# A softmax that streams through one core: three loads of 32 rows for six of 16, two stores of 32 rows, and VectorE's steps in another order

## The chip, the core and the metric

The kernel runs on one core of one Trainium2 chip. The metric is device time in microseconds (us); a kernel's time is the median of its runs. Of the core's engines, VectorE (DVE in the profile), ScalarE (ACT) and GpSimd (POOL) compute here, and SyncE's queue (SPq) issues all transfers between device memory (DRAM) and the on-chip memory (SBUF). TensorE isn't used.

## The reference

Softmax over the last axis of x, which has the shape 16 x 1024 x 512 in float32:

```python
x_max = np.max(x, axis=-1, keepdims=True)
exp_x = np.exp(x - x_max)
return exp_x / np.sum(exp_x, axis=-1, keepdims=True)
```

These are 16,384 independent rows of 512 elements. x has 33.55 MB and the output as much; both must cross the DMA engines once, 67.11 MB in all.

## The kernel before

**Tiling.** Each of the 128 partitions handles 128 rows, numbered 0 to 127 in each partition. Eight rows of all partitions make a *group* (`GROUP`, 128 x 4096 elements, 2.10 MB), so there are 16 groups, g = 0 to 15, and group g has the rows 8g to 8g + 7. The SBUF tensor `held` has room for 96 rows per partition, 12 groups (`RING`); rows 96 to 127 reuse the places of rows 0 to 31. All work is done in place in `held`.

**Transfers.** `BLOCKS` (line 21) says how rows in DRAM are dealt to partitions: in a block of n rows per partition, partition p has n consecutive rows of DRAM, which is n x 2 KB in one run. Before, each block has 16 rows, and so each DMA moves 16 rows of all partitions: 4.19 MB in 128 runs of 32 KB. `ORDER` (line 22) is SyncE's program, a list written by hand: "L" is a load (line 126) and "S" a store (line 152). SyncE does it strictly in this order. The first `AHEAD` entries, six loads, are issued at once (lines 133 to 135; `AT_HEAD` puts the first of them ahead of the start barrier). The rest (lines 139 to 154) wait before they are issued:

- a store waits until all groups in its rows are scaled (semaphores `scaled`, one per group);
- a load into reused places waits until every store that reads these places has landed (`stored`, one per store).

All DMAs go through one queue, in the order of their issue. A DMA that waits on SyncE holds back all that follow it in `ORDER`, though not those issued before it, which are still moving.

**Compute.** A group goes through four steps:

- M, on VectorE: `reduce_max` with the sign turned (line 164), 128 x 4096 to 128 x 8, after its load has landed (line 162);
- on ScalarE, in a loop over the groups in order (lines 190 to 203): eight activations of one row each, exp(x - max), in place, each with the row's sum as a by-product (line 195);
- on VectorE, once ScalarE is done with the group (line 169): the reciprocal of the eight sums (line 170);
- the multiply of the group by its reciprocals (line 172), either on GpSimd (called P) or on VectorE (called V).

`VECTOR` (line 44) is VectorE's program, again written by hand and done strictly in this order. "M5" is the max of group 5; "P5" is the reciprocal of group 5 on VectorE, and then GpSimd does the multiply; "V12" is the reciprocal and the multiply, both on VectorE. So GpSimd's multiplies come in the order of the P entries, and none starts before VectorE has reached its P entry. In before, groups 0 to 11 are scaled on GpSimd and 12 to 15 on VectorE.

Of the kernel before, what the change touches and what calls it, by code (L numbers as in the profile page):

```python
# [1 line left out]

# [4 lines left out]

F32 = mybir.dt.float32
EXP = mybir.ActivationFunctionType.Exp
AX = mybir.AxisListType.X  # L10

GROUP = 8
GROUPS = 16
RING = 12 * GROUP

BLOCKS = [(0, 16), (16, 32), (32, 48), (48, 64), (64, 80), (80, 96), (96, 112), (112, 128)]
ORDER = [
    ("L", (0, 16)),
    ("L", (16, 32)),
    ("L", (32, 48)),
    ("L", (48, 64)),
    ("L", (64, 80)),
    ("L", (80, 96)),
    ("S", (0, 16)),
    ("S", (16, 32)),  # L30
    ("S", (32, 48)),
    ("L", (96, 112)),
    ("L", (112, 128)),
    ("S", (48, 64)),
    ("S", (64, 80)),
    ("S", (80, 96)),
    ("S", (96, 112)),
    ("S", (112, 128)),
]
AHEAD = 6  # L40

VECTOR = """
    M0 M1 P0 M2 P1 M3 P2 M4 P3 M5 P4 M6 P5 M7 P6 M8 P7 M9 P8 M10 P9 M11
    P10 M12 P11 M13 V12 M14 V13 M15 V14 V15
"""

AT_HEAD = {mybir.EngineType.SP: 1}

def loads_at_the_head(nc):

    main, body = nc.main_func.blocks[0], nc.main_func.blocks[1]
    for engine, count in AT_HEAD.items():
        loads = [
            i
            for i in body.instructions
            if i.engine == engine and type(i).__name__ == "InstDMACopy"  # L60
        ][:count]
        barrier = next(
            n
            for n, i in enumerate(main.instructions)
            if i.engine == engine and type(i).__name__ == "InstDrain"
        )
        for load in loads:
            body.instructions.remove(load)
        main.instructions[barrier:barrier] = loads


@with_exitstack
def kernel(
    ctx: ExitStack,
    tc: tile.TileContext,
    x: bass.AP,
    out: bass.AP,
):
    nc = tc.nc
    nc.at_finalize(loads_at_the_head)  # L80
    P = nc.NUM_PARTITIONS

    d = x.shape[-1]
    x_rows, out_rows = x.flatten_outer_dims(), out.flatten_outer_dims()
    assert x_rows.shape[0] == GROUPS * GROUP * P

    def in_dram(rows, a, b):

        first, last = next(k for k in BLOCKS if k[0] <= a and b <= k[1])
        block = rows[first * P : last * P].rearrange("(p r) d -> p r d", p=P)  # L90
        return block[:, a - first : b - first, :]

    held = nc.alloc_sbuf_tensor("held", [P, RING, d], F32).ap()
    shift = nc.alloc_sbuf_tensor("shift", [P, GROUPS * GROUP], F32).ap()
    sums = nc.alloc_sbuf_tensor("sums", [P, GROUPS * GROUP], F32).ap()
    recip = nc.alloc_sbuf_tensor("recip", [P, GROUPS * GROUP], F32).ap()

    loads = [k for what, k in ORDER if what == "L"]
    stores = [k for what, k in ORDER if what == "S"]
    loaded = {k: nc.alloc_semaphore(f"loaded{k[0]}") for k in loads}  # L100
    scaled = [nc.alloc_semaphore(f"scaled{g}") for g in range(GROUPS)]
    stored = {k: nc.alloc_semaphore(f"stored{k[0]}") for k in stores}
    maxed = nc.alloc_semaphore("maxed")
    expd = nc.alloc_semaphore("expd")
    to_pool = nc.alloc_semaphore("to_pool")
    to_vector = nc.alloc_semaphore("to_vector")

    def take(engine, semaphore, n):

        engine.wait_ge(semaphore, n).then_inc(semaphore, -n)  # L110

    def rows(a, b):
        assert a // RING == (b - 1) // RING
        return held[:, a % RING : (b - 1) % RING + 1, :]

    def meets(k, a, b):
        return k[0] < b and a < k[1]

    def group(g):
        return g * GROUP, (g + 1) * GROUP  # L120

    def stats(t, g):
        return t[:, g * GROUP : (g + 1) * GROUP]

    def load(k):
        copy = nc.sync.dma_start(out=rows(*k), in_=in_dram(x_rows, *k))
        copy.then_inc(loaded[k], 16)
        return copy

    with tc.manual_schedule():
        for _, k in ORDER[:AHEAD]:
            tc.no_tile_sem_insts.add(load(k).ins.name)
    tc.close()
    tc.compile()  # L137

    taken, done = set(), set()
    for what, k in ORDER[AHEAD:]:  # L140
        if what == "L":
            for s in stores:
                if meets(s, k[0] - RING, k[1] - RING) and s not in taken:
                    take(nc.sync, stored[s], 16)
                    taken.add(s)
            load(k)
        else:
            for g in range(GROUPS):
                if meets(k, *group(g)) and g not in done:
                    take(nc.sync, scaled[g], 1)  # L150
                    done.add(g)
            nc.sync.dma_start(out=in_dram(out_rows, *k), in_=rows(*k)).then_inc(
                stored[k], 16
            )


    seen = set()

    def rowmax(g):
        for k in loads:  # L160
            if meets(k, *group(g)) and k not in seen:
                take(nc.vector, loaded[k], 16)
                seen.add(k)
        nc.vector.reduce_max(  # L164
            out=stats(shift, g), in_=rows(*group(g)), axis=AX, negate=True
        ).then_inc(maxed, 1)

    def scale(g, engine, ready):
        take(nc.vector, expd, 1)
        nc.vector.reciprocal(out=stats(recip, g), in_=stats(sums, g)).then_inc(ready, 1)  # L170
        take(engine, ready, 1)
        engine.tensor_mul(  # L172
            out=rows(*group(g)),
            in0=rows(*group(g)),
            in1=stats(recip, g).unsqueeze(2).to_broadcast([P, GROUP, d]),
        ).then_inc(scaled[g], 1)

    for step in VECTOR.split():
        what, g = step[0], int(step[1:])
        if what == "M":  # L180
            rowmax(g)
        elif what == "V":
            scale(g, nc.vector, to_vector)
        else:
            scale(g, nc.gpsimd, to_pool)


    nc.scalar.preload_act_table(EXP)  # L188

    with nc.scalar.Fori(0, GROUPS) as i:  # L190
        take(nc.scalar, maxed, 1)
        for r in range(GROUP):
            row = held[:, bass.ds(i % (RING // GROUP) * GROUP + r, 1), :]
            at = bass.ds(i * GROUP + r, 1)
            act = nc.scalar.activation(  # L195
                out=row,
                in_=row,
                func=EXP,
                bias=shift[:, at],
                scale=1.0,  # L200
                accum_out=sums[:, at],
            )
        act.then_inc(expd, 1)


    for k in stores:
        if k not in taken:
            take(nc.sync, stored[k], 16)


# [1 line left out]
_INS = ['x']  # L212
_OUTS = [((16, 1024, 512), 'float32')]


# [23 lines left out]
```

## Time and profile before

| what | us |
|---|---|
| median of three runs (lowest, highest) | 160.07 (159.98, 160.23) |
| the profiled execution | 160.14 |
| its span, first to last instruction or landing | 158.8 |
| busy: VectorE, ScalarE, GpSimd | 90.6, 92.0, 84.0 |

The profiled execution is 1.3 us longer than the span, for what lies around the program. A time within the profile counts from the span's start. The span doesn't end with a compute instruction but with the landing of the last store.

The trace tells for each DMA when SyncE issued it and how long it then took to land. In the order of issue (us; the numbers in brackets are the rows per partition):

| DMA | issued | issue to landing | landed |
|---|---|---|---|
| load (0,16) | 0.0 | 12.2 | 12.2 |
| load (16,32) | 0.8 | 21.1 | 21.9 |
| load (32,48) | 1.2 | 30.4 | 31.6 |
| load (48,64) | 1.6 | 39.7 | 41.3 |
| load (64,80) | 2.2 | 48.9 | 51.0 |
| load (80,96) | 2.6 | 58.8 | 61.4 |
| store (0,16) | 37.5 | 33.6 | 71.1 |
| store (16,32) | 51.5 | 29.4 | 80.9 |
| store (32,48) | 65.4 | 25.4 | 90.8 |
| load (96,112) | 71.3 | 29.0 | 100.3 |
| load (112,128) | 81.0 | 29.1 | 110.1 |
| store (48,64) | 81.5 | 38.3 | 119.8 |
| store (64,80) | 93.3 | 36.3 | 129.6 |
| store (80,96) | 112.3 | 27.1 | 139.4 |
| store (96,112) | 125.6 | 23.5 | 149.1 |
| store (112,128) | 140.9 | 17.9 | 158.8 |

Most of the time from issue to landing is spent behind the DMAs ahead in the queue. The difference of two consecutive landings is what one DMA takes of the engines.

Of the compute engines, the groups of instructions with the mean length of one:

| line, engine, step | count | mean ns |
|---|---|---|
| L164 VectorE, max of a group | 16 | 4399 |
| L195 ScalarE, Exp of one row | 128 | 712 |
| L172 GpSimd, multiply of a group | 12 | 7015 |
| L172 VectorE, multiply of a group | 4 | 4570 |
| L170 VectorE, reciprocal | 16 | 201 |

The early steps in order of time: VectorE starts M0 at 12.33, right after the first landing; ScalarE starts the Exp of group 0 at 17.11, that of group 1 at 22.76; reciprocal 0 starts at 23.00 and reciprocal 1 at 28.64; GpSimd's first multiply starts at 23.46, and eleven follow one another without a gap for 76.76 us.

In the lines of a timeline the columns are start, length, engine, line, operation and tiles with their shapes.

### The profile page before, as it was taken

What the parts mean: (1) busy time and instruction counts of PE and PEld (TensorE: products, weight loads), DVE (VectorE), ACT (ScalarE), POOL (GpSimd) and SP (SyncE); (2) the same over time, 40 slices, a digit from 0 to 9 for tenths busy, and PEclk for the clock granted to TensorE, in tenths of its full rate; (3) what the DMA queues carried; (4) which work ended last, traced back from release to release, by engine and by line L of the source; (5) the groups of instructions that cost most, each with busy time, mean ns of one, the idle gap of its engine ahead of it and who ended that gap; (6) DMA issues with size and microseconds to landing.
All of it is one profiled execution on the core that took longest, in us unless ns stands there. A gap on an engine that the chain in (4) does not pass through costs nothing. (4 is left out here: it accounts for less than half of the span.)

```text
span 158.8 us, 747 instructions
## 1 busy us (share of the span) xinstructions
DVE 90.6 (57%) x36; ACT 92.0 (58%) x257; POOL 84.0 (53%) x16
## 2 busy tenths in 40 slices
DVE  0008959777977977887700000795999998640000
ACT  0300699999999999999993000059934929200000
POOL 0000009999999999999999999259200000000000
DMA  7999999999999998999999999999999999999996
GB/s 264 470 454 396 413 487 421 396 454 470 396 396 487 437 396 380 413 396 454 470 396 421 462 437 396 446 479 396 421 446 454 396 437 473 413 404 454 446 413 264
DMA packets 2305, 67.12 MB, mean 423 GB/s; under 512 B 256, under 2 KB 256, under 8 KB 256
## 3 DMA queue, kind: packets, MB, share of 16 engines
q1 hardware_dynamic: 2304, 67.11, 98.9%
q14 instruction: 1, 0.01, 0.0%
HBM read 33.55 MB, written 33.55 MB: 423 GB/s over the span
## 5 line engine op out<-in xcount | busy, mean ns | idle before, releaser
L195 ACT ACTIVATE held<-held,shift x128 | 90.3, 712 | 40.0 <-ACTq L110 40.0
L172 POOL TENSOR_TENSOR held<-held,recip 128x4096 f32<-128x4096 f32 x12 | 83.8, 7015 | 28.0 <-POOLq L110 28.0
L164 DVE TENSOR_REDUCE shift<-held 128x8 f32<-128x4096 f32 x16 | 70.3, 4399 | 33.2 <-DVEq L110 33.2
L195 ACT ACTIVATION_READ_ACCUMULATOR held<-held,shift x128 | 24.6, 192 | 0.0
L172 DVE TENSOR_TENSOR held<-held,recip 128x4096 f32<-128x4096 f32 x4 | 18.3, 4570 | 0.6
L170 DVE RECIPROCAL recip<-sums 128x8 f32<-128x8 f32 x16 | 3.2, 201 | 16.5 <-DVEq L110 16.5
L188 ACT ACT_TABLE_LOAD x1 | 1.3, 1283 | 3.9 <-PEq L137 3.9
L223 POOL MEMSET const-float32-0.0<- 128x1 f32 x1 | 0.1, 98 | 0.2 <-issue 0.2
L223 POOL MEMSET const-uint8-127<- 128x1 uint8 x1 | 0.1, 102 | 0.0
L223 POOL MEMSET const-bfloat16-1.0<- 128x1 bf16 x1 | 0.1, 101 | 0.0
L223 POOL MEMSET const-float32-1.0<- 128x1 f32 x1 | 0.1, 98 | 0.0
## 6 DMA issues: line engine op xcount, KB each, us to landing
held<-in_x_dram SPq DMA_DIRECT2D x8, 4096.0 KB, 29.7
out_dram<-held SPq DMA_DIRECT2D x8, 4096.0 KB, 28.3
```

Source lines behind the costliest of these rows:

```text
L164: nc.vector.reduce_max(out=stats(shift, g), in_=rows(*group(g)), axis=AX, negate=True).then_inc(maxed, 1)
L170: nc.vector.reciprocal(out=stats(recip, g), in_=stats(sums, g)).then_inc(ready, 1)
L172: engine.tensor_mul(out=rows(*group(g)), in0=rows(*group(g)), in1=stats(recip, g).unsqueeze(2).to_broadcast([P, GROUP, d]),).then_inc(scal ...
L188: nc.scalar.preload_act_table(EXP)
L195: act = nc.scalar.activation(out=row, in_=row, func=EXP, bias=shift[:, at], scale=1.0, accum_out=sums[:, at],)
L223: nc = _bacc.Bacc("TRN2", target_bir_lowering=False, num_devices=1)
```

## The change

The blocks become 32 rows. The first six loads become three, of 32 rows per partition (8.39 MB in runs of 64 KB). Two stores, (0,32) and (64,96), move 32 rows each; the other four, and the two loads into reused places, keep 16 rows, which are now half of a block: per partition a run of 32 KB out of 64 KB. The bytes and the order of the rows in SyncE's queue are the same.

The semaphores follow. Store (0,32) waits for the groups 0 to 3 (before, store (0,16) waited for 0 and 1); store (64,96) waits for the groups 8 to 11. Both loads into reused places wait for store (0,32) as a whole. The first load's landing is what M0 to M3 wait for, the second that of M4 to M7, the third that of M8 to M11.

In VectorE's order, groups 3 and 10 are scaled on VectorE (V3, V10), and groups 12 and 13 on GpSimd (P12, P13). P4 stands behind V3 and P11 behind V10, and in three places two or three maxima follow one another (M0 M1 M2, M5 M6, M12 M13). GpSimd still has 12 multiplies and VectorE four. Nothing else differs; behind the shorter lists, all lines of the kernel have numbers lower by five.

```diff
-BLOCKS = [(0, 16), (16, 32), (32, 48), (48, 64), (64, 80), (80, 96), (96, 112), (112, 128)]
+BLOCKS = [(0, 32), (32, 64), (64, 96), (96, 128)]
 ORDER = [
-    ("L", (0, 16)),
-    ("L", (16, 32)),
-    ("L", (32, 48)),
-    ("L", (48, 64)),
-    ("L", (64, 80)),
-    ("L", (80, 96)),
-    ("S", (0, 16)),
-    ("S", (16, 32)),
+    ("L", (0, 32)),
+    ("L", (32, 64)),
+    ("L", (64, 96)),
+    ("S", (0, 32)),
     ("S", (32, 48)),
     ("L", (96, 112)),
     ("L", (112, 128)),
     ("S", (48, 64)),
-    ("S", (64, 80)),
-    ("S", (80, 96)),
+    ("S", (64, 96)),
     ("S", (96, 112)),
     ("S", (112, 128)),
 ]
-AHEAD = 6
+AHEAD = 3

 VECTOR = """
-    M0 M1 P0 M2 P1 M3 P2 M4 P3 M5 P4 M6 P5 M7 P6 M8 P7 M9 P8 M10 P9 M11
-    P10 M12 P11 M13 V12 M14 V13 M15 V14 V15
+    M0 M1 M2 P0 M3 P1 M4 P2 V3 P4 M5 M6 P5 M7 P6 M8 P7 M9 P8 M10 P9 M11
+    V10 P11 M12 M13 P12 M14 P13 M15 V14 V15
 """
```

## The prediction, as it was put on record before the changed kernel ran

> **What bounds it now.** I read the page's DMA rows first, then bandwidth by stretch, then SyncE's queue, and last the compute engines' timelines. Of the page:
>
> ```profile
> DMA  7999999999999998999999999999999999999996
> ...
> q1 hardware_dynamic: 2304, 67.11, 98.9%
> ...
> DVE 3%; issue 0%
> ```
>
> The DMA engines are full in every slice but the first and the last, while no compute engine is busy above 58% of the span. The third line, the chain of work that ended last, is blind here: it ends with VectorE's last multiply at 140.8 us and doesn't see that the span ends 18 us later with a store. The sum over stretches (time, DVE, ACT and POOL busy, clock, DMA share, GB/s) gives the sizes:
>
> ```profile
> 0.00:4.00 4.00, 0.00 (x0) 0.07 (x1) 0.20 (x4) 1.00 0.77 262
> 4.00:56.00 52.00, 35.90 (x14) 40.10 (x112) 32.54 (x5) 1.00 1.00 434
> 56.00:62.00 6.00, 4.56 (x2) 6.00 (x17) 6.00 (x2) 1.00 1.02 377
> 62.00:155.00 93.00, 50.12 (x20) 45.81 (x130) 45.23 (x7) 1.00 1.00 432
> ```
>
> Transfers run at 432 to 434 GB/s wherever the queue is full, so a 4.19 MB DMA takes 9.7 us and 67.11 MB take 155. The dip at 56 to 62 is the change from loads to stores: (434 - 377) x 6 / 434 = 0.8 us. So time can only be lost where SyncE's queue runs dry. When SyncE issues (start, us, count):
>
> ```profile
> 0.00 3.13 SPq L126 DMA_DIRECT2D held<-in_x_dram  x6
> 37.54 28.23 SPq L152 DMA_DIRECT2D out_dram<-held  x3
> 71.28 10.02 SPq L126 DMA_DIRECT2D held<-in_x_dram  x2
> 81.48 59.76 SPq L152 DMA_DIRECT2D out_dram<-held  x5
> ```
>
> Every DMA of before is issued long before its predecessor lands (table above): the first store at 37.5, while loads land until 61.4. That is over 20 us of cover, and it hides all compute. The price of a dry queue is in the first load: issued at 0.0 on an idle queue, it lands at 12.2, of which 9.7 is transfer. So a DMA keeps the queue full only if it is issued 2.5 us before its predecessor lands; later, it costs its lateness one for one.
>
> **The change part by part.**
>
> *Three loads for six.* Same bytes, same order. SyncE's issues fall by three (some 0.4 us each on SyncE's queue), which lay beside the first load: nothing. Two consecutive landings (71.1 and 80.9 of the first two stores) stand 9.7 us apart, which is 4.19 MB at 432 GB/s, so a boundary between queued DMAs costs nothing that shows, and five fewer boundaries gain nothing. A run of 64 KB per partition in place of 32 KB is in no row; I bound its effect at 1% of the 97 us that five 8.39 MB DMAs take, up or down (1 us), and take nothing, by the two stretches at 434 and 432.
>
> What changes is when data is usable. M0 waits for 8.39 MB, not 4.19: it starts at 12.33 + 9.7 = 22.0. The second load lands at 21.9 + 19.4 = 41.3, the third at 60.7.
>
> *VectorE's order and the merged store (0,32).* This store waits for groups 0 to 3, three on GpSimd (P0, P1, P2) and V3 on VectorE. Durations from the rows of before: a reduce starts 4.33 us after the one before it; the first Exp row follows its reduce's start by 4.8 (17.11 - 12.33); a group's reciprocal starts 5.9 us after its first Exp row (23.00 - 17.11), then one per 5.64; the multiply starts 0.46 after the reciprocal on GpSimd and 0.35 on VectorE; a GpSimd multiply takes 6.98 (76.76 / 11). So:
> M0, M1, M2 from 22.0 to 35.05; reciprocal 0 at 35.05 (ScalarE was done at 32.7, so the third reduce ahead of it costs 2.3); P0 at 35.5, P1 at 42.5, P2 from 49.46 to 56.45. M3 from 35.2; M4 waits for the second load, 41.4 to 45.8; reciprocal 2 at 45.8, in time for P2. Exp of group 3 is done in time for reciprocal 3 at 22.0 + 4.8 + 5.9 + 3 x 5.64 = 49.6, and V3 starts at 49.95: half a microsecond after P2 has begun. What VectorE's multiply costs beside GpSimd's shows once in before:
>
> ```profile
> 111.45 5.00 DVE L172 TENSOR_TENSOR held<-held,recip 128x4096 f32<-128x4096 f32 x1
> ...
> 121.04 4.43 DVE L172 TENSOR_TENSOR held<-held,recip 128x4096 f32<-128x4096 f32 x1
> ...
> 130.05 4.43 DVE L172 TENSOR_TENSOR held<-held,recip 128x4096 f32<-128x4096 f32 x1
> ```
>
> ```profile
> 105.16 7.01 POOL L172 TENSOR_TENSOR held<-held,recip 128x4096 f32<-128x4096 f32 x1 [4.94 <-POOLq L110]
> ```
>
> GpSimd's last multiply runs until 112.17. V12 starts beside it at 111.45 and takes 0.57 us more than its fellows, which have GpSimd idle; it ends 4.28 us after GpSimd's end, about its whole own length. So in the 0.72 us of overlap V12 got little or nothing done, while the reduces beside GpSimd keep their 4.4 us. I read this as V12 standing still until GpSimd is through. V3 then stands from 49.95 to 56.45 and ends at 56.45 + 4.28 to 4.43, say 60.75; the store is issued 0.1 later (as 37.54 follows the second GpSimd multiply's end, 23.46 + 2 x 6.98 = 37.42), 60.85.
>
> The Trainium skill (SBUF — State Buffer, section "Who interferes with whom") says that a VectorE instruction with two SBUF inputs and a GpSimd instruction that reads SBUF contend for one port pair, and that whichever starts first holds it for its whole instruction. The single short overlap here would also fit a slowdown in proportion, 0.57 lost of 0.72; by that, V3 would end at 59.5 and the sum would be 160.7 rather than 162.0. The lock is what I go by, since V12's end fits it within 0.15 us.
>
> The queue needed this store by 60.7 - 2.5 = 58.2. It comes 2.65 us late, and the store lands at 60.85 + 2.5 + 19.4 = 82.75, where before the same bytes had landed at 80.9. The 0.8 us of the change to stores is inside the 2.5, so the loss against before is **1.9 us**.
>
> *What queues behind V3.* On VectorE reciprocal 4 and with it P4, M5, M6 and P5; GpSimd idles from 56.45 to 61.2, a stall that wasn't there. P4 ends at 68.2. M5 starts at 60.9, M6 at 65.3; Exp 5 follows, reciprocal 5 at 71.6, P5 ends at 79.0: store (32,48) is issued at 79.15, needed by 82.75 - 2.5 = 80.25. It holds, with 1.1 us. Both loads of the last block wait for store (0,32) alone, and are issued at 82.8 behind store (32,48) (landing 92.4): in time, and they land at 102.1 and 111.8 (before 100.3 and 110.1).
>
> *V10 and the store (64,96).* P6, P7, P8 and P9 follow without gaps, P9 from 100.0 to 107.0. V10 is ready at 100.15, stands again, ends at 111.25; reciprocal 11, then P11 from 111.75 to 118.75. The store is issued at 118.9; store (48,64), which is ready by 93, lands at 121.5, so the need is by 119.0. Margin 0.1 us: I cost it at nothing, but all later slips cost in full. After it P13 ends at 136.5 (need 138.4) and V15 at 145.7 (need 148.1). The 4.7 us that V15 ends later is covered.
>
> *Sum.* Profiled execution of before 160.14 (span 158.8 plus 1.3 around it); plus 1.9 is 162.0. The median of the runs, 160.07, is lower by 0.07.
>
> **The rivals.**
> *The queue doesn't run dry (not slower).* If V3 ran freely beside P2 it would end at 54.4, and P2, at 56.45, would release the store at 56.6, 1.6 us ahead of the need. All later margins grow, and the time is that of before: 160.1. The point that decides is a release before 58.2. For it: only one overlap of 0.72 us speaks for the standing. Against it: the 0.57 has no other cause in the rows. Chance 0.12.
> *In proportion:* V3 ends at 59.5, 0.7 us late against before: 160.8. Chance 0.10.
> *V3 first.* If P2 started after V3, V3 would end at 54.4 and P2, standing, at 61.4: 162.6. Needs 0.5 us against my schedule; I count it with the forecast.
> *A second dry spell* at store (64,96), where the margin is 0.1: P11 one microsecond later makes 163.0. Chance 0.06.
> *64 KB runs:* 1% better or worse moves the first landing by 0.2 us and the two big stores by 0.2 each: 161.4 or 162.6 with the dry queue, inside the forecast; as a gain of 1 us without the dry queue 159.1. Chance of the latter 0.04.
> *A start paid per DMA.* If each DMA cost part of its 2.5 us start, five fewer would gain up to 12 us: 148. Landings 9.7 us apart at 432 GB/s deny it; chance 0.01. The Trainium skill (DMA: Bandwidth & Descriptors, "Anatomy of one DMA — SWDGE (gpsimd) path") gives about 2 us fixed per DMA, for GpSimd's path; worked out, an estimate of 10 us less. This trace shows it only at the idle start.
>
> **How the numbers follow.** Forecast 162.0 with 0.67 (161.4 to 162.8), the others as above. Leaving out the gains below 160.2, most of the undisturbed case, and half of the second dry spell gives the range 160.2 to 163.2. 0.2% is 0.3 us, about what a measurement of this kernel can tell from no change: slower 0.67 + 0.10 + 0.06 = 0.83, same 0.12, faster 0.05.
>
> **What would show it.** V3 as a VectorE multiply of about 10.8 us ending 4.3 us after GpSimd's third; store (0,32) issued near 60.9 and landing 21.9 later; a dip in the GB/s near 61; V10 about 11 us long; GpSimd idle 4.7 us after its third multiply. The forecast is wrong if V3 takes about 4.4 us, if the first reduce doesn't start near 22.0, or if the loads' rate differs from 434 GB/s.

## The result

The changed kernel takes 162.77 us (median of six runs, 162.42 to 162.97) beside 160.03 of before (159.95 to 160.23). It is slower by 2.7 us; 162.0 was forecast. The ratio on record is 1.0163, with a 95% interval of 1.0153 to 1.0173 (the two medians alone give 1.0171). The profiled execution took 162.62 us with a span of 161.3.

The page's DMA rows after:

```profile
DMA  8996996996996969699699999998999899799996
...
q1 hardware_dynamic: 1584, 67.11, 97.9%
```

The share of the queue has fallen from 98.9% to 97.9% of a longer span. (The 6 that comes back in the first half is no idle time: packets of 64 KB are counted where they start.) Bandwidth by stretch shows where time went (columns as in the prediction's table of stretches):

```profile
56.00:62.00 6.00, 6.00 (x3) 0.00 (x0) 1.43 (x2) 1.00 0.81 350
59.60:61.50 1.90, 1.90 (x3) 0.00 (x0) 0.58 (x1) 1.00 0.00 0
...
88.00:112.00 24.00, 21.36 (x8) 16.96 (x49) 19.43 (x4) 1.00 1.01 401
112.00:155.00 43.00, 28.36 (x10) 22.68 (x64) 20.14 (x3) 1.00 1.01 435
```

The same last three stretches of before:

```profile
59.60:61.50 1.90, 1.81 (x1) 1.90 (x6) 1.90 (x1) 1.00 0.64 276
...
88.00:112.00 24.00, 9.57 (x5) 6.79 (x19) 19.06 (x3) 1.00 1.01 436
112.00:155.00 43.00, 26.81 (x9) 16.11 (x46) 0.17 (x1) 1.00 0.99 428
```

There are two places. From 59.6 to 61.5 no packet starts: the dry queue of the forecast. By the packets of the trace, the last ones of the loads end between 59.6 and 60.1 and the store's first one starts at 61.6, so that each DMA engine idles for 1.8 us. From 88 to 112 the engines look full (share 1.01), but move 401 GB/s in place of 436: (436 - 401) x 24 / 436 = 1.9 us that the forecast knew nothing of. (This count is coarse, since a packet counts where it starts; the landings below give 1.5.) VectorE, GpSimd and SyncE's queue around the dry spell:

```profile
49.54 0.20 DVE L165 RECIPROCAL recip<-sums 128x8 f32<-128x8 f32 x1 [3.72 <-DVEq L105]
49.89 10.74 DVE L167 TENSOR_TENSOR held<-held,recip 128x4096 f32<-128x4096 f32 x1
60.55 0.19 DVE L165 RECIPROCAL recip<-sums 128x8 f32<-128x8 f32 x1
```

```profile
35.38 20.96 POOL L167 TENSOR_TENSOR held<-held,recip 128x4096 f32<-128x4096 f32 x3 [34.95 <-POOLq L105]
60.92 7.02 POOL L167 TENSOR_TENSOR held<-held,recip 128x4096 f32<-128x4096 f32 x1 [4.57 <-POOLq L105]
```

```profile
60.73 18.38 SPq L147 DMA_DIRECT2D out_dram<-held  x2
81.70 1.63 SPq L121 DMA_DIRECT2D held<-in_x_dram  x2
92.71 52.53 SPq L147 DMA_DIRECT2D out_dram<-held  x4
```

V3 lasts 10.74 us and ends at 60.63, 4.3 us after GpSimd's third multiply (35.38 + 20.96 = 56.34). The store follows at 60.73; the second DMA of that row, store (32,48), is issued at 78.76. GpSimd meanwhile idles for 4.57 us, because P4 stands behind V3.

A DMA lands in 16 parts. Below is the time at which the first part of each landed, in the trace (us). The two kernels on the right are experiments of the next section.

| DMA | before | changed | order V2 V3 | before, store (32,48) late |
|---|---|---|---|---|
| last of the early loads | 60.98 | 59.99 | 60.42 | 61.19 |
| store that ends with row 32 | 80.36 | 81.32 | 80.14 | 80.56 |
| store (32,48) | 90.34 | 91.64 | 90.23 | 91.06 |
| load (96,112) | 99.76 | 101.35 | 99.51 | 101.04 |
| load (112,128) | 109.47 | 111.97 | 109.36 | 111.45 |
| store (48,64) | 119.14 | 121.68 | 119.03 | 121.14 |
| last store | 157.80 | 160.35 | 157.68 | 159.86 |

In what follows, the *lead* of a DMA is the time from its issue to the landing of the first part of the DMA ahead of it in the queue. In the changed kernel store (0,32) has none (it is issued 0.74 us after that landing), and store (32,48) has 2.6 us.

The changed kernel is behind before by 0.96 at the first store, 1.59 two DMAs later, 2.50 at the last load, and 2.55 at the end. The dry spell itself is worth 1.0; the rest comes at two *changes of direction*, from store (32,48) to the loads and from the loads to store (48,64). The packets show how: of store (32,48), the last one of every engine takes 0.75 us more than the usual 1.21, and around the end of the last load 25 packets take longer, together 1.1 us per engine. In before, no packet at these two changes takes 0.1 us more than usual.

### The profile page after: what moved, and what is told of

Read it like the earlier page. It is cut to its first block, busy times and chain, and to the rows that moved or that the text cites. A ratio compares the mean times of both kernels' runs of the same rounds, so it can differ in the third digit from the quotient of the medians.

```text
span 161.3 us, 737 instructions
## 1 busy us (share of the span) xinstructions
DVE 105.0 (65%) x36; ACT 91.9 (57%) x257; POOL 84.1 (52%) x16
## 3 DMA queue, kind: packets, MB, share of 16 engines
q1 hardware_dynamic: 1584, 67.11, 97.9%
## 5 line engine op out<-in xcount | busy, mean ns | idle before, releaser
L167 DVE TENSOR_TENSOR held<-held,recip 128x4096 f32<-128x4096 f32 x4 | 33.2, 8298 | 0.6
L190 ACT ACTIVATION_READ_ACCUMULATOR held<-held,shift x128 | 23.8, 186 | 0.0
```

What stands on the lines that cost most here:

```text
L167: engine.tensor_mul(out=rows(*group(g)), in0=rows(*group(g)), in1=stats(recip, g).unsqueeze(2).to_broadcast([P, GROUP, d]),).then_inc(scal ...
L190: act = nc.scalar.activation(out=row, in_=row, func=EXP, bias=shift[:, at], scale=1.0, accum_out=sums[:, at],)
```

## The experiments

Theory A: V3 stands for GpSimd, the queue runs dry, and that is the loss. Rival B: the bigger transfers themselves make the changes of direction slow. The later theories H, K1, K2, R and S are stated where they were formed. Each edit is against the changed kernel unless said otherwise. Ratios are against runs of before taken together with the experiment (medians of 160.13 to 160.27). A trace exists of one run of each kernel.

**The first store cut in two.**

```diff
-    ("S", (0, 32)),
+    ("S", (0, 16)),
+    ("S", (16, 32)),
```

> The changed kernel with its first store cut in two, (0,16) and (16,32); all else as changed. Two theories. A, the dry queue: V3 stands for GpSimd's multiply, so the 32-row store is issued at 60.7, after the loads have drained, and the 1.8 us in which no packet moves (59.6 to 61.6) are what is lost; the two later slow changes between stores and loads (0.75 us near 89.6 and 1.1 us near 109 in the profile of the changed kernel) follow from the shifted issue times. B, the big transfers: these two slow changes come from 32-row blocks and half-block runs themselves and stay without a dry queue. Here store (0,16) waits for P0 and P1 alone and is issued near 49.5; V3 still takes about 10.7 us, and store (16,32) is issued near 60.7, with 9 us of cover. A: 160.0 to 160.4. B: 161.6 to 162.0.

162.43 us (161.57 to 163.13), ratio 1.0134 (1.0103 to 1.0165). That lies above both forecasts, and A as it stands does not explain it: the queue never ran dry (store (0,16) was issued at 49.6, store (16,32) at 60.9, 9.7 us ahead), and yet nearly all the loss stayed. It lies at the same two changes; from 88 to 112 this kernel moves 404 GB/s. Of the DMAs that still have a change behind them only store (32,48) was close: issued at 78.9, with a lead of 1.35 us.

**The reciprocals of VectorE's multiplies in PSUM.**

```diff
+    recip_v = nc.alloc_psum_tensor("recip_v", [P, GROUPS * GROUP], F32).ap()
...
+        to = recip_v if engine is nc.vector else recip
-        nc.vector.reciprocal(out=stats(recip, g), in_=stats(sums, g)).then_inc(ready, 1)
+        nc.vector.reciprocal(out=stats(to, g), in_=stats(sums, g)).then_inc(ready, 1)
...
-            in1=stats(recip, g).unsqueeze(2).to_broadcast([P, GROUP, d]),
+            in1=stats(to, g).unsqueeze(2).to_broadcast([P, GROUP, d]),
```

> The changed kernel with the reciprocals of VectorE's own multiplies (V3, V10, V14, V15) written to and read from PSUM in place of SBUF, so that these multiplies have one input in SBUF; the order and all transfers as changed. If V3 stands because both engines want the same read path to SBUF, V3 takes about 4.5 us, ends near 54.4, and GpSimd's P2 (end 56.4) releases the store at 56.5, ahead of the drain at 59.6. A, the dry queue: 160.0 to 160.5. B, the big transfers: 161.6 to 162.0. If V3 stands for another reason (the shared output buffer, the semaphore), it keeps its 10.7 us and the time stays at 162.8.

160.34 us (159.98 to 161.69), ratio 1.0018 (0.9999 to 1.0037). V3 in this kernel's timeline:

```profile
49.62 0.21 DVE L167 RECIPROCAL recip_v<-sums 128x8 f32<-128x8 f32 x1 [3.74 <-DVEq L106]
49.98 4.42 DVE L169 TENSOR_TENSOR held<-held,recip_v 128x4096 f32<-128x4096 f32 x1
```

It starts as before beside P2, and takes 4.42 us in place of 10.74. Only the place of 128x8 numbers changed. So it is the second input from SBUF that makes V3 stand; once that is gone, so is the loss. The rule of the Trainium skill that the prediction drew on (SBUF — State Buffer, "Who interferes with whom") speaks of two inputs in SBUF; this run agrees, with 4.42 against 10.74. The 32-row transfers are all still there, against B.

**Six loads of half a block.**

```diff
-    ("L", (0, 32)),
-    ("L", (32, 64)),
-    ("L", (64, 96)),
+    ("L", (0, 16)),
+    ("L", (16, 32)),
...
-AHEAD = 3
+AHEAD = 6
```

> The changed kernel with six loads of 16 rows (each half of a 32-row block, runs of 32 KB) in place of three of 32; both 32-row stores and VectorE's order as changed. M0 starts at 12.3 again, P2 ends near 46.8, V3 stands and ends near 51, and store (0,32) is issued there, 9 us ahead of the drain. A, the dry queue: 160.0 to 160.4, although V3 and V10 still take about 11 us. B, the big transfers: the 32-row stores and the half-block runs are still there, so 161 to 162.

160.51 us, ratio 1.0017 (1.0008 to 1.0025). The store is issued at 52.1, 8.9 us ahead. V3 did not take 11 us, as I had expected, but 4.8: with the earlier loads VectorE gets to it at 40.2, half a microsecond before GpSimd's P1 ends, and holds up P2 instead, GpSimd's third multiply, which takes 11.2 us in place of 7.0. B falls for the 32-row stores and the half-block runs: they cost at most 0.25% (the upper end of the interval).

**Another order, all transfers as changed.**

```diff
-    M0 M1 M2 P0 M3 P1 M4 P2 V3 P4 M5 M6 P5 M7 P6 M8 P7 M9 P8 M10 P9 M11
-    V10 P11 M12 M13 P12 M14 P13 M15 V14 V15
+    M0 M1 P0 M2 P1 M3 M4 V2 V3 P4 M5 M6 P5 M7 P6 M8 P7 M9 P8 M10 P9 M11
+    P10 P11 M12 M13 P12 M14 P13 M15 V14 V15
```

> The changed kernel with another order on VectorE: P0 and P1 earlier, groups 2 and 3 both on VectorE (V2, V3), group 10 on GpSimd: M0 M1 P0 M2 P1 M3 M4 V2 V3 P4 M5 M6 P5 M7 and so on, P10 P11 in place of V10 P11. All transfers as changed. P0 starts at 33.1, P1 ends at 47.1; V2 stands for it and ends near 51.4, V3 runs alone to 56.3, and store (0,32) is issued at 56.4, 1.8 us ahead of the 58.2 that I took as its due time. A, the dry queue: 160.0 to 160.5. B, the big transfers: 161.6 to 162.0.

160.30 us, ratio 1.0014 (1.0001 to 1.0028). Both multiplies run alone, and store (0,32) is issued at 56.69, with a lead of 3.7 us (its stretches stand last):

```profile
47.48 4.43 DVE L167 TENSOR_TENSOR held<-held,recip 128x4096 f32<-128x4096 f32 x1
...
52.16 4.43 DVE L167 TENSOR_TENSOR held<-held,recip 128x4096 f32<-128x4096 f32 x1
```

```profile
56.69 18.38 SPq L147 DMA_DIRECT2D out_dram<-held  x2
81.04 1.55 SPq L121 DMA_DIRECT2D held<-in_x_dram  x2
88.67 51.15 SPq L147 DMA_DIRECT2D out_dram<-held  x4
```

```profile
62.00:86.00 24.00, 18.69 (x9) 24.00 (x70) 20.29 (x4) 1.00 0.97 421
88.00:112.00 24.00, 14.34 (x8) 18.95 (x55) 24.00 (x5) 1.00 1.01 431
```

So the transfers of the change are harmless by themselves, 32-row loads included. Its order on VectorE is harmless with six loads (the run before). The loss needs both: data that come late, in three loads, and a V3 that stands for P2 just when the store is due. What stayed open was the first experiment: slow changes without a dry queue. Four kernels were made for that, with the theories H (the split stores), K1 (a store issued after the packets have turned to loads) and K2 (a store issued shortly before it is due).

**The split store, with the reciprocals in PSUM** (both edits above).

> The kernel with the split first store (162.4, though its queue never ran dry) with the reciprocals of VectorE's multiplies in PSUM, so that V3 and V10 don't stand and store (32,48) is issued near 73.7 and store (48,64) near 87.6, as in the fast kernel with the unsplit store. What is open is why a change of direction in the queue is slow: the last packets of store (32,48) and of the second late load take 0.5 to 1.1 us longer in the changed kernel and in the split one, and at most 0.3 in the fast three. H, the splitting itself: stores of half a block beside 32-row loads are slow, and the time stays at 162.4. K, issue times: the slow changes come from stores issued late, after the packets have turned to loads (48,64) or just before they are needed (32,48); the time is 160.1 to 160.5.

160.39 us, ratio 1.0020 (1.0010 to 1.0030). H falls. Store (32,48) is issued at 73.5, with a lead of 7.0 us, and the changes are quick.

**Store (48,64) late**, against the order V2 V3: `meets(k, *group(g))` becomes true for g = 8 as well where k is (48, 64).

> The kernel with V2 V3 (160.3) in which store (48,64) waits for group 8 as well, so that it is issued near 95.5 in place of 88.7; it is due only near 107, and nothing else moves but store (64,96), not at all. K1, a store issued after the packets have turned to loads pays at the changes: the last packets of store (32,48) and of the second late load take 0.6 and 0.9 us longer, 161.4 to 162. K2, only store (32,48) being issued shortly before it is due matters: 160.3.

160.21 us, ratio 1.0003 (0.9994 to 1.0011), with the store issued at 95.6. K1 falls.

**Store (32,48) late by a mark**, against the order V2 V3 (the first two lines show a part of the `VECTOR` line).

```diff
-M7 P6 M8 P7
+M7 P6 M8 T0 P7
...
+            if k == (32, 48):
+                take(nc.sync, late, 1)
...
+        elif what == "T":
+            nc.vector.reciprocal(out=mark, in_=stats(recip, 0)).then_inc(late, 1)
```

> The kernel with V2 V3 (160.3) in which store (32,48) waits for a mark that VectorE sets after M8 (a reciprocal of 128x8 into a tile of its own, 0.2 us), so that it is issued near 77.7 in place of 74.7; store (48,64) stays near 88.7. It is still 2.4 us ahead of its predecessor's first landing, as 2.6 in the changed kernel. K2, a store issued shortly before it is due makes the changes after it slow: 161.0 to 162. K1, only the issue of store (48,64) matters: 160.3.

160.72 us, ratio 1.0052 (1.0025 to 1.0078), but the eleven runs spread from 160.03 to 162.18, where the twelve without the mark spread from 160.00 to 160.96. The profiled one, 160.32, lies near the lower end and shows no slow change, with a lead of 2.7 us; none of the long runs has a trace. The store seems to be at the edge; the run is inconclusive by itself.

**Store (48,64) late in the kernel of before**: the same edit in before, for g = 8 and 9.

> The kernel of before in which store (48,64) waits for the groups 8 and 9 as well, so that it is issued at 93.4 in place of 81.5, together with store (64,80), which was issued at 93.3 anyway. All transfers are of 16 rows, nothing runs dry, and store (48,64) is due near 107. K1: slow changes at the end of store (32,48) and of the last load, 0.6 and 0.9 us: 161.4 to 162. K2, and H: 160.1.

160.19 us, ratio 0.9997 (0.9989 to 1.0006), with the store issued at 93.4. K1 falls for 16-row transfers too.

**The mark after reciprocal 7**, so that the lead of store (32,48) is 1.1 us.

```diff
-M8 T0 P7 M9
+M8 P7 T0 M9
```

> The kernel with V2 V3 and the mark, the mark now set after reciprocal 7, so that store (32,48) is issued near 78.9, 1.2 us ahead of its predecessor's first landing (80.1) in place of 2.7; store (32,48) is still in the queue before that landing. The run with 2.7 us gave times from 160.0 to 162.2. K2, a store issued within about 3 us of its predecessor's landing makes the changes of direction after it slow: with less lead it is slow in nearly all runs, 161.3 to 163. If the spread of that run had another reason: 160.2 to 160.8.

162.71 us (161.37 to 163.25), ratio 1.0146 (1.0114 to 1.0178). The store was issued at 78.8. The profiled run is one of the shorter ones, 161.58; its stretches:

```profile
62.00:86.00 24.00, 18.76 (x10) 24.00 (x70) 20.29 (x4) 1.00 0.97 418
88.00:112.00 24.00, 14.28 (x8) 18.82 (x55) 24.00 (x5) 1.00 1.00 406
```

The queue is full all along, and up to 86 it is as quick as with the order V2 V3 (421); from 88 to 112 it moves 406 GB/s in place of 431. K2 holds: 1.6 us less lead cost 2.0 us (162.71 beside 160.72).

**M5 ahead of V3 in the changed kernel**, so that the dry spell stays and store (32,48) is early.

```diff
-P2 V3 P4 M5 M6 P5
+P2 M5 V3 P4 M6 P5
```

> The changed kernel with M5 ahead of V3 in VectorE's order, all else as changed. V3 still stands for P2 and ends at 60.6, store (0,32) is still issued at 60.7 and the queue still runs dry, for about 1.8 us near 60; but Exp 5 is done by 60.7, P5 follows P4 at once and ends near 74.9, and store (32,48) is issued near 75.0, 6 us ahead of its predecessor's landing in place of 2.6. A with K2, two separate costs: the dry queue alone stays, 160.9 to 161.4. A alone, all of the 2.7 us being the dry queue's: 162.5 to 162.9.

162.63 us (162.54 to 162.87), ratio 1.0149 (1.0136 to 1.0163). I had expected 160.9 to 161.4; the time is that of A alone. Its stretches:

```profile
59.60:61.50 1.90, 1.90 (x3) 1.05 (x4) 0.62 (x1) 1.00 0.00 0
...
88.00:112.00 24.00, 19.46 (x7) 16.49 (x48) 24.00 (x4) 1.00 1.02 406
```

The dry spell is there as in the changed kernel, store (32,48) is issued at 75.0, with a lead of 6.3 us, and the changes after 88 are slow all the same (the first parts of load (96,112) and of the last load land at 101.42 and 112.01, as in the changed kernel). So the two are not separate costs: a dry queue makes the later changes slow just as a late DMA does. I read it as the extreme case of a DMA that comes too late; no run tests that reading further. One of them is enough, and the second adds little (162.77 with both). In the changed kernel it is the dry queue: a store (32,48) with a lead of 2.7 us and no dry queue gave only 160.72.

**Store (32,48) late in the kernel of before**: it waits for the groups 6 and 7 as well.

> The kernel of before in which store (32,48) waits for the groups 6 and 7 as well, so that it is issued near 79.4 in place of 65.4, 1.0 us ahead of its predecessor's first landing (80.4). All transfers are of 16 rows and the queue doesn't run dry. K2 as a rule of the queue: slow changes at the end of store (32,48) and of the last load, 161.3 to 163. If K2 needs the 32-row transfers: 160.0 to 160.4.

162.12 us (161.70 to 163.56, the profiled one being the longest), ratio 1.0107 (1.0092 to 1.0122). Its queue and two stretches:

```profile
37.76 42.18 SPq L152 DMA_DIRECT2D out_dram<-held  x3
80.05 1.61 SPq L126 DMA_DIRECT2D held<-in_x_dram  x2
81.71 61.64 SPq L152 DMA_DIRECT2D out_dram<-held  x5
```

```profile
62.00:86.00 24.00, 13.74 (x7) 23.14 (x66) 24.00 (x4) 1.00 1.01 437
88.00:112.00 24.00, 8.81 (x3) 4.67 (x13) 17.15 (x3) 1.00 0.98 392
```

The first of these stretches in before (the second, at 436 GB/s, stands above):

```profile
62.00:86.00 24.00, 13.74 (x7) 22.91 (x66) 24.00 (x4) 1.00 1.00 430
```

The third store is now issued at 79.6 (37.76 + 42.18 less its own length), 1.0 us ahead of 80.56. Nothing stalls there: 437 GB/s up to 86. The 16-row transfers of before then become slow at the same two changes (right column of the table: 0.2 behind before at 80, 2.0 at the last load). The last of the 16 parts are later still in this trace: that of the last load lands at 113.75 in place of 110.03. So it is no matter of 32 rows, of VectorE or of GpSimd. One more DMA moves with the edit: load (96,112), behind the store in `ORDER`, is issued at 80.05 in place of 71.28. That isn't the cause: with the order V2 V3 it is issued at 81.04, and nothing is slow.

**A late store with no change of direction after it**, in before: store (80,96) waits for a mark behind V13.

```diff
-V13 M15 V14
+V13 T0 M15 V14
...
+            if k == (80, 96):
+                take(nc.sync, late, 1)
...
+            nc.vector.reduce_max(
+                out=mark[:, :4], in_=rows(96, 100), axis=AX
+            ).then_inc(late, 1)
```

> The kernel of before in which store (80,96) waits for a mark that VectorE sets after a max of 4 rows (2.2 us, into a tile of its own) behind V13, so that it is issued near 127.7 in place of 112.3, 1.1 us ahead of its predecessor's first landing (128.8). Only stores follow it. R, a store issued into a queue that has almost run out makes the later changes of direction slow, and costs nothing else while it is still ahead of the landing: no change follows, so 160.0 to 160.5. S, such a store makes the queue slow by itself, whatever follows: 161.3 to 163.

160.21 us, ratio 1.0003 (0.9994 to 1.0012), with the store issued at 127.8, a lead of 0.9 us:

```profile
127.76 0.85 SPq L156 DMA_DIRECT2D out_dram<-held  x2
```

S falls, R holds: the late issue costs nothing by itself, only at later changes.

## Why the prediction was right, and where it was wrong

*Right, step by step.* M0 starts at 21.95 (forecast 22.0), M4 at 41.30 (41.4). V3 starts at 49.89 (49.95), lasts 10.74 (10.8), and the store is issued at 60.73 (60.85). GpSimd idles 4.57 us (4.7) after its third multiply. V10 lasts 11.02 (11). VectorE ends at 144.8 (145.7), covered, as forecast. The step that carried the forecast, V12's 5.00 us beside 4.43 read as standing and not as sharing, holds for V3: it ends 4.29 us after GpSimd's multiply, about its whole own length, where sharing in proportion would have ended it at 59.5 and not at 60.63. That the second input from SBUF is why, is shown by the run with PSUM. No second dry spell came: store (64,96) was issued at 118.24, and the first part of store (48,64) landed only at 121.68. Of the rivals, free running and sharing in proportion are out. Two small sums don't agree within the forecast, and nothing hangs on them: by its own times V15 ends 4.9 us later and not 4.7 (4.0 was measured), and sharing in proportion is given as 160.7 and as 160.8.

*Wrong in size: the price of the dry queue.* The forecast charged a DMA that is issued on an idle queue 2.5 us beside its transfer, read from the first load. Store (0,32) took 20.9 us from issue to landing; two of before's steps of 9.7 are 19.4, so 1.5 lay around it. In the first load the first packets take 0.7 us longer; the store's do not. So the store landed at 81.6 and not at 82.75: against before it was 0.96 us late in its first part and 0.7 in its last, not 1.9. The engines' idle time fits this: they idled for 1.8 us, and the change from loads to stores, some 0.8 us in before, cost nothing behind the dry spell.

*Wrong: "a boundary between queued DMAs costs nothing that shows" and "later, it costs its lateness one for one".* The first was read from two stores in a row, where no direction changes. The second ends the bill with the late landing. The runs show 1.5 us more: behind the dry queue the next two changes of direction cost 0.6 and 0.9 us, which are 0 in before. A DMA that is late without letting the queue run dry has the same effect: leads of 1.0 to 1.35 us were slow in three kernels, 2.7 us gave both, and 3.4 us and more were quick in every trace without a dry queue. The forecast asks for 2.5 us before the last part of the predecessor lands. At 3.5 us by that measure (the lead of 2.7) the runs already spread, so 2.5 is too little ahead of a change. The forecast gave store (32,48) a margin of 1.1 us ("it holds"), of which 0.35 was left (issued at 78.76, predecessor landed at 81.61); that this store was close was, by the run with M5 ahead of V3, not needed for the loss.

The two errors have opposite signs, 0.9 too much and 1.5 too little, and so the sum of 1.9 came near the 2.5 of the two spans. The direction, the cause and the place of the first stall are shown; nearness of the sum is partly luck.

*What stays open:* why the engines are quick at a change of direction in one case and not in the other. That they look ahead in the queue and lose this when it runs short would fit, but no run shows it. The edge isn't sharp either: single runs of kernels with longer leads were long too (161.08 and 161.69 of twelve with the reciprocals in PSUM, leads of 4.1 us and more; 161.22 of twelve with the split store and PSUM, 7.0 and more), and none of them has a trace. In before the first change, near 59, is slow too (the 0.8 us of the prediction), though its store was issued at 37.5; the queue had started empty at 0, and the later changes are quick.

None of the versions beats before: the best with the 32-row transfers takes 160.21, with 1 within its interval.

## What to carry to other kernels

Where one queue of DMAs bounds a kernel, work out for each DMA its lead, the time from its issue to its predecessor's landing, and keep it well above 3 us ahead of changes between loads and stores (in the kernels at 160.2 to 160.5 it was 3.4 or more for every DMA that a change still followed; of twelve runs at 4.1, two still took over 161); a full DMA row on the page doesn't show that it holds. A store that waits for more rows waits for the slowest engine among them: look for what stands there, such as a VectorE multiply with two SBUF inputs beside a GpSimd multiply, which took 10.7 us here in place of 4.4. Put one of the inputs into PSUM, or order the steps so that the two don't meet.

## What the runs showed of the hardware that was not expected

- A store issued 1.0 to 1.35 us ahead of the first landing of its predecessor leaves hardly a gap (the engines idle for 0.06 us each or less), and yet costs about 2 us later, where the queue turns from stores to loads and back (162.12 to 162.71 in three kernels); with a lead of 0.9 us and no such turn after it, it costs nothing (160.21). At 2.7 us the runs spread between both.
- Packets of 64 KB are as quick as those of 32 KB: the loads of 8.39 MB land 19.35 us apart, two of 4.19 MB 19.42. Five fewer DMAs brought no gain that shows (160.21 in the best kernel that has them, beside 160.13 of before).
